# Sums of the output projection's weights formed in the first pass on GpSimd and loaded ready-made into the projection

## The chip, the cores and the metric

One Trainium2 chip, one core of it. The metric is device time in microseconds (us) of one execution of the whole program, the median of several executions. TensorE (PE) does the matmuls, VectorE (DVE), ScalarE (ACT) and GpSimd (POOL) the elementwise work, and all transfers are issued by SyncE (SP), one after the other.

## The reference, cut to what matters

Two layers of a decoder trunk over 2048 rows of 1024 columns, in fp32. Each layer normalises x, projects it, runs gated linear attention (GLA, 4 heads) and causal attention (MLA, 4 heads) beside each other, gates both, joins them and projects back onto x:

```
for l in range(2):
    h = rmsnorm(x, norm_g[l]);  u = h @ w_in[l]
    gla = rmsnorm(gla_mix(q, k, v, log_a)) * silu(g_gla)      # 512 columns, weighted by gla_norm_g
    mla = block_causal_attention(rope(q), rope(k), v) * silu(g_mla)   # 512 columns
    x = x + concat([gla, mla]) @ w_out[l]                     # w_out: 1024 x 1024
```

## The kernel before

A layer is four stages on the time line of the profile: a first pass over the rows (GLA; layer 0 from 0 to 345 us, layer 1 from 1152 to 1460), a second pass (gates and the MLA's projections, to 610 and 1730), the attention (`phase_b`, to 980 and 2107) and the output projection (`phase_c`, to 1152 and 2279). PE's order is written by hand in `block` and in the list of jobs of `phase_c`. The order of the other engines is set when the program is built, by a scheduler that puts each instruction where it reckons that its inputs are ready; on the chip every engine then takes its instructions strictly in that order, and SP issues its transfers in order too.

**The first pass** goes over 16 tiles of 128 rows in 8 pairs. A pair has six blocks of matmuls: `mi` (low-rank gates and latents) of both tiles, then `qk` and `v` of each. Beside them ACT and DVE make what the next matmuls need: `lah` and `ls_a` are the log gates, `ep`, `en`, `es` their exponentials, `kq` the scaled keys, `vs` and `vr` the values, `hT` the rounded rows. Every fp32 operand goes to PE as a high and a low part (`..._h`, `..._l`): ACT copies the high part, a second engine subtracts it to get the low one, and three matmuls (L97 to L99) make one product. In layer 0 ACT also sums the squares of later rows (`xn`, L405), each loaded into one buffer. GpSimd has nothing to do in this pass.

**The output projection** multiplies by the 2 x 2 blocks of `w_out` in Winograd's form of Strassen's method: seven products in place of eight, for each of two halves of the rows (p = 0, 1). Four products have sums of weight blocks as their weights: S1, N2, S3 and S4; two have a block itself (A11, A12), one has A22. A product is 48 matmuls of 128x512 (L1428, `co`). In p = 0 the order is M1 (A11), M2 (A12), M5 (S1), M6 (N2), M7 (S3), M3 (S4), M4 (A22). The sums are made in p = 0 itself: `s1`, `n2`, `s3`, `s4` load the blocks again (`ws`, 256 KB each), add them on DVE and POOL and split them with `wput` (L1204, L1205, L1207, L1208), one 128-row piece k after the other, a product or so ahead of their use. In the same stretch DVE also adds up the left operands: `y` (L1265 on ACT, L1266 on DVE), with `yr` and `rc` the stored rows and L1281 their sums, and takes the results out of PSUM (`xc`, L1333).

The names in the tiles: `kv` (matmuls from `vr` and `kq`) is the update of the GLA state, `od` the stored GLA output, `xt` rows loaded for later tiles, `osn` a staging tile.

## Time and profile before

| | |
|---|---|
| time, median of three runs | 2282.6 us (2280.12 to 2284.39) |
| time of the profiled execution | 2284.48 us |
| span in its profile | 2282.5 us |
| PE busy | 2205.2 us, 97% of the span |
| DVE busy | 1634.0 us, 72% |
| ACT busy | 1367.0 us, 60% |
| POOL busy | 422.2 us, 18% |
| granted clock of PE, mean | 0.989 |

The profile shows one execution; the span runs from the first instruction to the last, and 1.98 us of the execution's time lie outside it. Busy shares are means over stages with different limits, so the rows below are taken by stage.

### The profile page before, as it was taken

The numbers are of one execution on the slowest core, as the hardware profiler recorded it, in microseconds if no ns is written. First come the engines' busy times: TensorE is split into PE (matmuls) and PEld (weight loads), VectorE is DVE, ScalarE is ACT, GpSimd is POOL, SyncE is SP. The second block draws the span as 40 slices with busy tenths as digits, with TensorE's granted clock in tenths as the row PEclk, the third lists the DMA queues.
The fourth block names the chain that finished last, engine by engine and source line by source line (L and its number), as shares of the span: only waits on it lengthen the run. The fifth ranks groups of instructions, "written<-read, shape, count | busy, mean of one in ns | idle before, by whom it ended". The sixth has DMA issues, their size and how long they took to land.

```text
span 2282.5 us, 37395 instructions
## 1 busy us (share of the span) xinstructions
PE 2205.2 (97%) x12405; PEld 1899.2 (83%) x12405; DVE 1634.0 (72%) x4759; ACT 1367.0 (60%) x3706; POOL 422.2 (18%) x621
## 2 busy tenths in 40 slices
PE   7999999999999999998999999999999999999989
PEld 5778888888899988876878888888888989988677
DVE  5665557676788887677867667677777888885774
ACT  6655456776777777632445555667777777775321
POOL 0000002334312123224000000034342122122320
PEclk8999999999999999999999999999999999999999
DMA  5411114443411111168531011244434111111863
GB/s 192 134 48 42 43 51 145 133 136 101 137 37 51 31 47 52 47 222 268 176 107 41 29 42 43 64 151 140 124 100 125 29 54 36 39 55 48 271 217 112
DMA packets 180481, 223.66 MB, mean 98 GB/s; under 512 B 13936, under 2 KB 124608, under 8 KB 179264
## 3 DMA queue, kind: packets, MB, share of 16 engines
q1 hardware_dynamic: 180288, 221.28, 30.5%
q8 instruction: 98, 1.61, 0.3%
q14 instruction: 95, 0.78, 0.1%
HBM read 158.31 MB, written 62.91 MB: 97 GB/s over the span
## 4 chain that ended last, share of the span: by engine, by line
PE 81%; DVE 7%; ACT 5%; DMA 4%; issue 1%; SPq 1%; POOL 0%; ACTq 0%; DVEq 0%; POOLq 0%
PE co L1428 10%; PE tp L94 9%; PE o L1059 3%; PE sp L984 3%; PE o L1058 3%; PE sp L987 3%; PE o L1057 3%; PE sp L988 3%; PE sp L986 2%; PE sp L985 2%; PE mg L99 2%; PE mg L97 2%; PE mg L98 2%; PE gt L99 2%; PE gt L98 2%; PE gt L97 2%
## 5 line engine op out<-in xcount | busy, mean ns | idle before, releaser
L995 DVE TENSOR_SCALAR_CACHE_REDUCE p<-sp 128x512 f32<-128x512 f32 (+5 forms) x304 | 173.2, 573 | 23.1 <-PE sp L988 19.6
L1037 ACT ACTIVATE ph<-tp 128x512 fp32r<-128x512 f32 x224 | 130.7, 594 | 80.5 <-PE tp L94 70.3
L1038 DVE TENSOR_TENSOR pl<-tp,ph 128x512 fp32r<-128x512 f32 x224 | 152.2, 687 | 35.9 <-ACT ph L1037 34.8
L1002 ACT ACTIVATE p<-p,nm 128x128 f32<-128x128 f32 (+15 forms) x128 | 153.8, 1202 | 32.8 <-DVE nm L1001 27.5
L1057 PE MATMUL o<-ph,v 128*128 128x256 f32 x576 | 167.6, 291 | 3.6 <-ACT ph L1037 3.2
L1059 PE MATMUL o<-pl,v 128*128 128x256 f32 x576 | 170.0, 295 | 1.0 <-DVE pl L1038 0.5
L94 PE MATMUL tp<-cst,p 128*128 128x128 f32 x1088 | 168.0, 276 | 2.0 <-ACT p L1002 1.0
L1058 PE MATMUL o<-ph,v 128*128 128x256 f32 x576 | 161.4, 280 | 0.0
L184 POOL TENSOR_TENSOR ropeu<-kpe,cos 128x256 f32<-128x256 f32 x8 | 6.3, 791 | 808.6 <-DMA on<-od 433.2
L984 PE MATMUL sp<-kn,q 128*128 128x512 f32 (+3 forms) x320 | 129.6, 405 | 8.4 <-ACT q L919 6.7
L94 PEld LDWEIGHTS tp<-cst,p 128*128 128x128 f32 x1088 | 126.3, 141 | 11.2 <-ACT p L1002 2.2
L1057 PEld LDWEIGHTS o<-ph,v 128*128 128x128 f32 x576 | 109.1, 189 | 9.4 <-ACT ph L1037 4.6
L985 PE MATMUL sp<-kn,q 128*128 128x512 f32 (+3 forms) x320 | 116.6, 365 | 0.0
L986 PE MATMUL sp<-kn,q 128*128 128x512 f32 (+3 forms) x320 | 116.3, 370 | 0.0
L987 PE MATMUL sp<-kr,q 128*128 128x512 f32 (+3 forms) x320 | 115.2, 367 | 0.4
L1059 PEld LDWEIGHTS o<-pl,v 128*128 128x128 f32 x576 | 109.3, 190 | 6.5 <-DVE pl L1038 2.1
L1016 POOL TENSOR_SCALAR gt<-gt,rl 128x128 f32<-128x128 f32 x128 | 80.1, 636 | 185.5 <-DVE rl L1014 90.9
L988 PE MATMUL sp<-kr,q 128*128 128x512 f32 (+3 forms) x320 | 114.4, 368 | 0.0
L1058 PEld LDWEIGHTS o<-ph,v 128*128 128x128 f32 x576 | 109.1, 189 | 2.5
L97 PE MATMUL vp<-wv_h,hT 128*128 128x512 f32 x256 | 108.2, 423 | 1.8 <-ACT wv_h L264 1.8
L97 PE MATMUL qk<-wqk_h,hT 128*128 128x512 f32 x256 | 108.2, 423 | 0.0
L97 PE MATMUL mi<-wmi_h,hT 128*128 128x464 f32 x256 | 99.7, 390 | 7.4 <-ACT wmi_h L264 7.4
(322 smaller groups left out, 7061.8 us busy)
## 6 DMA issues: line engine op xcount, KB each, us to landing
rc<-yd SPq DMA_DIRECT2D x64, 256.0 KB, 4.6
ws<-in_w_out SPq DMA_DIRECT2D x56, 256.0 KB, 5.3
qd<-qs SPq DMA_DIRECT2D x32, 384.0 KB, 2.9
gst<-qd SPq DMA_DIRECT2D x64, 192.0 KB, 2.5
xn<-in_x SPq DMA_DIRECT2D x16, 512.0 KB, 3.3
od<-osn SPq DMA_DIRECT2D x32, 256.0 KB, 2.1
hf<-in_xt SPq DMA_DIRECT2D x16, 512.0 KB, 3.3
on<-od SPq DMA_DIRECT2D x32, 256.0 KB, 2.8
```

Of the source, the lines that this page charges most:

```text
L94: T.transpose(o, i, ident[:k, :k])
L97: T.matmul(o, lhsT=lh, rhs=rh, start=start, stop=False)
L984: T.matmul(o, lhsT=qn[:, 0, ts_], rhs=kn[:, 0, k0:k1], start=True, stop=False)
L985: T.matmul(o, lhsT=qn[:, 0, ts_], rhs=kn[:, 1, k0:k1], start=False, stop=False)
L986: T.matmul(o, lhsT=qn[:, 1, ts_], rhs=kn[:, 0, k0:k1], start=False, stop=False)
L987: T.matmul(o, lhsT=qrr[:, 0, ts_], rhs=kr[:, c0:c1], start=False, stop=False)
L988: T.matmul(o, lhsT=qrr[:, 1, ts_], rhs=kr[:, c0:c1], start=False, stop=True)
L995: V.tensor_scalar(out=pt[:, c0:c0 + w], in0=sp[:, 0:w], scalar1=0.0, scalar2=-3e38, op0=ALU.add, op1=ALU.max, accum_out=mx[:, m:m + 1])
L1057: T.matmul(o[:, s], lhsT=vh, rhs=ph[:, j, s], start=(kb == 0), stop=False)
L1058: T.matmul(o[:, s], lhsT=vl, rhs=ph[:, j, s], start=False, stop=False)
L1059: T.matmul(o[:, s], lhsT=vh, rhs=pl[:, j, s], start=False, stop=(last and j == 1))
L1428: T.matmul(o, lhsT=a[:, k, cs], rhs=y[:, b, :], start=(fresh and k == 0 and c == 0), stop=(k == 3 and c == 2), skip_group_check=True)
```

## The change

The four sums are no longer formed in the projection. Instead, the first pass of each layer forms them in 16 rounds, of one 128-row piece and 128 columns each, on GpSimd: three rounds in each of the pairs 1 and 2 and two in each of the pairs 3 to 7, as the code is written. A round loads the four blocks' pieces into one buffer `wq` (`wr_load`, two transfers of 128 KB), forms the sums in place (`wr_sum`, five POOL instructions), splits them into a high part (a copy on ACT) and a low part (POOL), and stores both to a new scratch tensor `wd` in device memory (`wr_put`, two transfers of 256 KB). There is one `wq` buffer, so a round's loads wait for the stores of the round before. In the projection `wsums` loads each sum's high and low parts, 1 MB each: S1 and N2 at the end of `phase_b`, S3 and S4 in the first two products. The A22 jobs move from the fifth product to the fourth. Apart from that the negated sine table `nsin` goes: `rope` now ends in a subtraction and an addition of half width on POOL where it had one addition, and the small tile `w3` takes the place of other staging tiles, with `finish_w3` of layer 1 called in the projection of layer 0.

```diff
-        V.tensor_scalar(out=nsin, in0=sin, scalar1=-1.0, scalar2=None, op0=ALU.mult)
...
-        eng.tensor_tensor(out=w[:, :, 0:32], in0=i[:, :, 32:64], in1=ns, op=ALU.mult)
+        eng.tensor_tensor(out=w[:, :, 0:32], in0=i[:, :, 32:64], in1=s, op=ALU.mult)
         eng.tensor_tensor(out=w[:, :, 32:64], in0=i[:, :, 0:32], in1=s, op=ALU.mult)
-        eng.tensor_tensor(out=o, in0=u, in1=w, op=ALU.add)
+        eng.tensor_tensor(out=o[:, :, 0:32], in0=u[:, :, 0:32], in1=w[:, :, 0:32], op=ALU.subtract)
+        eng.tensor_tensor(out=o[:, :, 32:64], in0=u[:, :, 32:64], in1=w[:, :, 32:64], op=ALU.add)
...
+        wrounds, wr = [(k, c) for k in range(4) for c in range(4)], {}
+
+        def wr_load(i):
+            k, c = wrounds[i]
+            wr[i] = w1.tile([P, 2, 4, P], F32R, tag="wq", name="wq", bufs=1)
+            t = wr[i][:, 0].bitcast(F32)
+            for half in range(2):
+                r0 = half * 512 + k * P
+                dma(t[:, 2 * half:2 * half + 2, :],
+                    w_out[l][r0:r0 + P, :].rearrange("p (a b c) -> p a b c", a=2, b=4)[:, :, c, :])
+
+        def wr_sum(i):
+            t = wr[i][:, 0].bitcast(F32)
+            a11, a21, a12, a22 = (t[:, j, :] for j in range(4))
+            G.tensor_scalar(out=t[:, 0:2, :], in0=t[:, 0:2, :], scalar1=sm["glag"], scalar2=None, op0=ALU.mult)
+            G.tensor_tensor(out=a22, in0=a21, in1=a22, op=ALU.add)
+            G.tensor_tensor(out=a21, in0=a11, in1=a21, op=ALU.subtract)
+            G.tensor_tensor(out=a11, in0=a11, in1=a22, op=ALU.subtract)
+            G.tensor_tensor(out=a12, in0=a12, in1=a11, op=ALU.add)
+
+        def wr_put(i):
+            k, c = wrounds[i]
+            w = wr.pop(i)
+            A.activation(out=w[:, 1], in_=w[:, 0].bitcast(F32), func=AF.Copy)
+            G.tensor_tensor(out=w[:, 0], in0=w[:, 0].bitcast(F32), in1=w[:, 1].bitcast(F32), op=ALU.subtract)
+            for part in range(2):
+                dma(wd[l][:, part, :, k, c * P:(c + 1) * P], w[:, part].bitcast(F32))
...
+            for b0 in () if p == 0 else (0, 2, 4) if p < 3 else (0, 4):
+                i = wnext[0]
+                wnext[0] += 1
+                wj[b0] = {1: [go(wr_load, i)], 6: [go(wr_sum, i)]}
+                wj[b0 + 1] = {5: [go(wr_put, i)]}
...
             load_a1(1)
+            for name in ("S1", "N2"):
+                wsums(l, name)
...
+    def wsums(l, name):
+        b = ("N2", "S3", "S4", "S1").index(name)
+        wo[name] = unit([P, 4, 512], F32R, f"{name}h{l}"), unit([P, 4, 512], F32R, f"{name}l{l}")
+        for part in range(2):
+            dma(wo[name][part].bitcast(F32), wd[l][:, 1 - part, b])
...
-        def s1(k):
-            wmake("S1")
-            t, u = wload(1, k), wload(1, 4 + k)
-            V.scalar_tensor_tensor(out=u, in0=t, scalar=g, in1=u, op0=ALU.mult, op1=ALU.add)
-            wput("S1", k, u, G)
...
-        for j, f in enumerate((s1, n2, s3, s4, a22)):
-            for k in range(4):
-                at(0, j, k, go(f, k))
+        at(0, 0, 0, go(wsums, l, "S3"))
+        at(0, 1, 0, go(wsums, l, "S4"))
+        for k in range(4):
+            at(0, 3, k, go(a22, k))
```

In the program that is built, the rounds do not stand where the code has them. Three places show it. First ACT, at the end of the fourth pair of layer 1's first pass. Before, the last rows of the log gates (`lah`) are followed by the values (`vs`, `vr`) that the next `kv` matmuls take:

```order
L398 ACTIVATE xn<-xt 128x1024
L120 ACTIVATE ls_a<-ls_a 128x256
L509 ACTIVATE qkT<-tp 128x512
L512 ACTIVATE kq<-qkT 128x256
L456 ACTIVATE lah<-ls_a 128x256
L532 ACTIVATE vs<-vp,rt 128x512
L534 ACTIVATE vr<-vp,rt 128x512
L349 ACTIVATE hT<-xt 128x512 x2
L471 ACTIVATE ep<-bp 128x256
L472 ACTIVATE en<-bp 128x256
```

Now the copy of the sixteenth and last round stands between them:

```order
L399 ACTIVATE xn<-xt 128x1024
L121 ACTIVATE ls_a<-ls_a 128x256
L510 ACTIVATE qkT<-tp 128x512
L513 ACTIVATE kq<-qkT 128x256
L457 ACTIVATE lah<-ls_a 128x256
L617 ACTIVATE wq<-wq 128x512
L533 ACTIVATE vs<-vp,rt 128x512
L535 ACTIVATE vr<-vp,rt 128x512
L350 ACTIVATE hT<-xt 128x512 x2
L472 ACTIVATE ep<-bp 128x256
L473 ACTIVATE en<-bp 128x256
```

The row L617 is the only one that is new here. Of the 16 copies of layer 1, the first stands behind the first `lah` of the pass and this one behind the eighth; in layer 0 the first stands behind the first `lah`, the ninth behind the fourth `hT` pair and the sixteenth ahead of the seventh `vs`.

Second SP, in the first pass of layer 1. Before, it issues rows and GLA outputs alone (`xt`, `od`):

```order
L59 DMA xt<-xd_80 128x1024
L59 DMA od_114<-osn 128x512
L59 DMA od_115<-osn 128x512
L59 DMA xt<-xd_80 128x1024 x2
L59 DMA od_116<-osn 128x512
L59 DMA od_117<-osn 128x512
L59 DMA xt<-xd_80 128x1024
L59 DMA xt<-xd_81 128x1024
```

Now the loads and stores of the rounds stand between them, each `wq` load behind the `wd` stores of the round before and each `wd` store behind the copy on ACT and the subtraction on POOL:

```order
L59 DMA wq<-in_w_out 128x2x128 x2
L59 DMA wd_102<-wq 128x4x128 x2
L59 DMA xt<-xd_79 128x1024
L59 DMA wq<-in_w_out 128x2x128 x2
L59 DMA od_115<-osn 128x512
L59 DMA wd_102<-wq 128x4x128 x2
L59 DMA wq<-in_w_out 128x2x128 x2
L59 DMA wd_102<-wq 128x4x128 x2
L59 DMA wq<-in_w_out 128x2x128 x2
L59 DMA od_116<-osn 128x512
```

Every other row of this queue is now one whose turn comes only when a round has got that far.

Third DVE, at the start of layer 0's projection. Before, three `y` low parts stand ahead of the first results (`xc`), with the scaling of `ws` for S1 between them:

```order
L1069 TENSOR_TENSOR yT<-o,gT 128x256
L1266 TENSOR_TENSOR y<-rc,y 128x512 x3
L1333 TENSOR_TENSOR xc<-co,xc 128x512
L1221 SCALAR_TENSOR_TENSOR ws<-ws,pk 128x512
L1333 TENSOR_TENSOR xc<-co,xc 128x512 x2
L1221 SCALAR_TENSOR_TENSOR ws<-ws,pk 128x512
L1333 TENSOR_TENSOR xc<-co,xc 128x512
L1266 TENSOR_TENSOR y<-rc,y 128x512
L1266 TENSOR_TENSOR y<-yr,y 128x512
L1281 TENSOR_TENSOR yr<-rc,yr 128x512
```

Now the `ws` rows are gone, and the four results of M1 stand ahead of the first `y`:

```order
L1107 TENSOR_TENSOR yT<-o,gT 128x256
L212 TENSOR_TENSOR w3r<-w_12285,w3r 32x256
L1349 TENSOR_TENSOR xc<-co,xc 128x512 x4
L1282 TENSOR_TENSOR y<-rc,y 128x512 x4
L1282 TENSOR_TENSOR y<-yr,y 128x512
L1297 TENSOR_TENSOR yr<-rc,yr 128x512
L1282 TENSOR_TENSOR y<-yr,y 128x512
L1297 TENSOR_TENSOR yr<-yr,rc 128x512
L1297 TENSOR_TENSOR yr<-rc,yr 128x512
```

The first `y` (L1282, L1266 before) is what M2 waits for; it has moved behind four results.

## Rows read from the trace of the kernel before

**Rows 1.** Windows over the projections' first halves, one second half and one first pass.

```profile
core 0: us, PE busy (x) PEld busy (x) DVE busy (x) ACT busy (x) POOL busy (x), PEclk, DMA share, GB/s
980.00:1075.60 95.60, 84.32 (x340) 66.10 (x339) 70.44 (x91) 29.63 (x49) 36.28 (x24) 0.93 0.81 264
2107.20:2202.40 95.20, 82.73 (x339) 64.50 (x339) 72.52 (x92) 29.91 (x49) 35.72 (x24) 0.95 0.80 258
2202.40:2278.60 76.20, 76.20 (x337) 62.80 (x335) 41.00 (x65) 14.54 (x23) 0.00 (x0) 1.00 0.40 132
1168.00:1309.00 141.00, 137.39 (x755) 115.69 (x754) 94.92 (x305) 77.42 (x253) 0.00 (x0) 1.00 0.11 34
```

**Rows 2.** Waits from 975 to 1100 us: engine, line, releaser, us, times, longest.

```profile
PE co L1428 <- DVE S4l L1205: 4.0, 1, 4.0
...
PE co L1428 <- DVE S3l L1208: 2.5, 1, 2.5
...
PE co L1428 <- ACT y L1265: 1.6, 1, 1.6
```

**Rows 3.** Windows right behind two of these waits, columns as in rows 1.

```profile
1003.70:1017.00 13.30, 12.95 (x48) 9.91 (x49) 13.30 (x19) 3.71 (x7) 4.56 (x3) 0.87 0.96 296
1047.80:1062.00 14.20, 10.17 (x36) 8.20 (x36) 9.80 (x12) 5.03 (x9) 7.10 (x6) 0.76 0.83 250
```

**Rows 4.** DVE by form, 980 to 1076 us: count, busy us, mean ns, idle before.

```profile
L1333 DVE TENSOR_TENSOR xc<-co,xc 128x512 f32<-128x512 f32 x25 | 16.5, 678 | 2.0 <-PE co L1428 2.0
```

**Rows 5.** POOL by form over the span, columns as in rows 4.

```profile
L1016 POOL TENSOR_SCALAR gt<-gt,rl 128x128 f32<-128x128 f32 x128 | 80.1, 636 | 185.5 <-DVE rl L1014 90.9 <-DMA gt<-gd 39.3 <-PE tp L94 25.6
...
L187 POOL TENSOR_TENSOR ropew<-qr,nsin 128x128 f32<-128x128 f32 x32 | 23.7, 741 | 0.0
...
L1205 POOL TENSOR_TENSOR N2l<-ws,N2h 128x512 fp32r<-128x512 f32 x8 | 12.0, 1494 | 17.7 <-ACT N2h L1204 17.7
...
L1205 POOL TENSOR_TENSOR S1l<-ws,S1h 128x512 fp32r<-128x512 f32 x8 | 11.0, 1370 | 67.8 <-ACT S1h L1204 67.8
...
L187 POOL TENSOR_TENSOR ropew<-kpe,nsin 128x128 f32<-128x128 f32 x8 | 3.7, 461 | 0.0
```

**Rows 6.** DMA issues of tiles xd, then gt: issue to landing, us.

```profile
DMA to landing us min/median/max: 2.5/4.1/7.5
DMA to landing us min/median/max: 1.7/1.9/6.1
```

**Rows 7.** DMA issues from 1152 to 1300 us: KB each, median us to landing.

```profile
xd<-xc SPq DMA_DIRECT2D x1, 256.0 KB, 2.8
```

**Rows 8.** ACT by form, 65 to 121 us, columns as in rows 4.

```profile
L349 ACT ACTIVATE hT<-xt 128x512 fp32r<-128x512 f32 x6 | 3.4, 622 | 0.0
```

**Rows 9.** Timeline of ACT, layer 1: start, us, instruction, idle before and releaser.

```profile
1168.17 0.39 ACT L421 ACTIVATE jk<-mi 128x256 f32<-128x256 f32 x1 [0.92 <-DVE lr L417]
...
1306.37 0.40 ACT L456 ACTIVATE lah<-ls_a 128x256 fp32r<-128x256 f32 x1
1308.91 0.69 ACT L532 ACTIVATE vs<-vp,rt 128x512 f32<-128x512 f32 x1 [2.15 <-PE vp L99]
```

**Rows 10.** Timeline of ACT, layer 0.

```profile
69.69 1.06 ACT L405 ACTIVATE xn<-xn 128x1024 f32<-128x1024 f32 x1 [2.30 <-DMA xn<-in_x]
...
74.13 1.06 ACT L405 ACTIVATE xn<-xn 128x1024 f32<-128x1024 f32 x1 [3.29 <-DMA xn<-in_x]
...
117.96 1.14 ACT L349 ACTIVATE hT<-xt 128x512 fp32r<-128x512 f32 x2
...
186.86 0.69 ACT L532 ACTIVATE vs<-vp,rt 128x512 f32<-128x512 f32 x1 [2.39 <-PE vp L99]
```

**Rows 11.** Waits from 65 to 121 us.

```profile
ACT xn L405 <- DMA xn<-in_x: 16.7, 11, 3.3
```

**Rows 12.** Timeline of DVE, then of PE, around one update of the GLA state.

```profile
1267.91 0.69 DVE L535 TENSOR_TENSOR vr<-vs,vr 128x512 fp32r<-128x512 f32 x1 [1.44 <-ACT vr L534]
...
1269.83 0.28 PE L97 MATMUL kv<-vr,kq 128*128 128x256 f32 x1
```

More of the change, by code (lines that the diff above doesn't have):

```diff
@@ L76, in trunk @@
     sin = cp.tile([P, NT, 32], F32, name="sin")
-    nsin = cp.tile([P, NT, 32], F32, name="nsin")
     v3 = cp.tile([P, NT, 3], F32, name="v3")
@@ L86, in trunk @@
     yd = [dp.tile([P, KT, QD], F32, name=f"yd{q}") for q in range(NQD)]
+    wd = [dp.tile([P, 2, 4, 4, 512], F32, name=f"wd{l}") for l in range(DEPTH)]
     qd = [dp.tile([P, HEADS, 2, 192], F32, name=f"qd{g}") for g in range(NG)]
@@ L202, in layer_small @@
         r["gqk"] = lp.tile([P, 1], F32, name="gqk")
-        w3 = lp.tile([96, 256], F32, name="w3", bufs=1)
+        w3 = w3[0:96, 0:256]
         dma(w3, w3s[l])
@@ L659, in pass1 @@
                 dma(cst[:, 0:C_MASK], consts[:, 0:C_MASK])
-                layer_small(0)
+                layer_small(0, w1.tile([P, 512], F32, tag="osn", name="w3"))
                 for load, _ in pq:
@@ L726, in run @@
                 ts_ = slice(4 * b, 4 * b + 4)
-                rope(G, w2, kpe[:, ts_, :], kpe[:, ts_, :], 4, cos[:, ts_, :], sin[:, ts_, :], nsin[:, ts_, :],
+                rope(G, w2, kpe[:, ts_, :], kpe[:, ts_, :], 4, cos[:, ts_, :], sin[:, ts_, :],
                      "qr")
@@ L1183, in phase_c @@
             layer_g8(l + 1)
-            layer_small(l + 1)
+            layer_small(l + 1, wc.tile([P, 512], F32, tag="rc", name="w3", bufs=3))
+            smalls[l + 1]["finish_w3"]()
         g = smalls[l]["glag"]
```

40 lines of the change are left out of this document (12 added, 28 removed).

## The prediction

> **What bounds the kernel now.** I read the windows by stage first, then the waits inside the one stage that loses time, and last the order in which the trace's instructions will stand once the rounds are among them. In layer 1's first pass PE is busy 137.4 of 141 us, with POOL at 0 and ACT busy 77 [rows 1]: PE is the bound there, the others have room. In the second half of layer 1's projection PE is busy 76.20 of 76.20 us for seven products [rows 1], which is 10.89 us a product. The first half is the same work, but takes 95.6 us in layer 0 and 95.2 in layer 1 [rows 1]: 19.4 and 19.0 us are lost, 38.4 in all. The waits name what ends last there: S4's low part 4.0 us, S3's 2.5, the left operand y 1.6 [rows 2]. PE is busy for 84.3 us with work that needs 76.2 [rows 1]; the other 8 us are the clock, granted at 0.87 and 0.76 in the stretches right behind the stalls [rows 3], between its two levels of 1.2 and 2.4 GHz.
>
> **What the change takes away.** The sums leave the projection: S3's and S4's waits have no maker on DVE left, and what DVE, ACT and POOL did for them goes too, with 24 loads of 256 KB a layer; eight of 1 MB come, four of them issued before the half begins. I do not book all 38.4 us. Three things are late next. M2: DVE now takes M1's four results ahead of the first y, four rows of 0.68 us at a spacing of some 0.6 [rows 4]; that is 2.4 us, of which some 1.4 fall on PE. S4's low part is now a load that waits for M1's end, and SP holds a row for M2 behind it: about 1.0. M5's y is still made on DVE: 1.6 was lost before [rows 2]; I take 2.5, since results now stand between its rows. Each stall brings a lower clock: at 0.87 over 13.3 us that is 1.7 us, at 0.76 over 14.2 it is 3.4 [rows 3]; I take 3.5 for two milder drops. Left are 8.4 us a half, so the gain is 11.0 and 10.6; less 1 us, because the y copies on ACT now stand among the last of the attention's. Together **20 us**. The bounds: 10, if M5 and S3's load stay as late as S3 and S4 are now, and 37, if nothing of the kind is left.
>
> **What it adds in the first pass.** Sixteen rounds a layer, and they form a closed loop, because one buffer serves them all: the loads wait for the stores, the stores for POOL, POOL for the loads. No round stands in the trace of before, so I add one up from the nearest rows.
> - The subtraction that makes the low part, 128x512 on POOL: 1.43 us, between 1.37 and 1.49 [rows 5].
> - The store of 256 KB in runs of 512 bytes: the tile xd is stored in the same shape, 2.8 us when it is alone [rows 7], 2.5 at least [rows 6]; loaded stretches give up to 7.5, and I take 3.3 for a high end, since this pass moves only 34 GB/s [rows 1].
> - The first load, 128 KB: 64 KB in runs of 512 bytes land in 1.9 us [rows 6], 256 KB in 2.8; I take 2.2 (1.9 to 2.7). The second runs beside it and beside the scaling.
> - The scaling on POOL, 128x256: 128x128 takes 0.64 [rows 5]; I take 1.0 (0.64 to 1.1).
> - Four 128x128 operations, each on the result of the one before: 0.46 or 0.74 [rows 5], so 2.4 with 0.60 each (1.85 to 2.96).
> - ACT's copy of 128x512: 0.62 [rows 8].
> - Six hand-overs. A row load that follows ACT shows the size: from 69.69 + 1.06 to 74.13 are 3.38 us [rows 10] for a landing of about 3.3 us, so below 0.1 each; 0.4 in all.
>
> Sum: 1.43 + 2.8 + 2.2 + 1.0 + 2.4 + 0.62 + 0.4 = **10.8 us a round**, with 9.3 and 12.5 as ends. This would be hidden if the copies stood far enough apart in ACT's order, since ACT waits in that order. They don't. In layer 1 the first stands just ahead of the row at 1168.17 and the sixteenth ahead of that at 1308.91 [rows 9]: 140.7 us for 15 rounds, 9.4 each. In layer 0 the ninth stands behind the hT pair that ends at 119.1 and the sixteenth ahead of 186.86 [rows 10]: 67.8 us for 7, 9.7 each; before the ninth they stand further apart. Behind a late copy are queued the values, the gates and the keys of the tile at hand, and PE's next kv matmuls wait for the values: vr is ready at 1268.60 and used at 1269.83 [rows 12], so the slack is 1.2 us, once. A PE that is 97% busy in this stretch makes nothing up.
> - Layer 1: 15 x 10.8 - 140.7 - 1.2 = 20.1 us lost.
> - Layer 0: 7 x 10.8 - 67.8 - 1.2 = 6.6 us lost.
> - Another 2 us in layer 0 before the ninth round: SP stands still between a store and the next load, with row loads (xn) queued behind it, and ACT already waits for those 11 times, 16.7 us in all [rows 11]. That is also the nearest case of the same mechanism: a loop of one buffer, 4.4 us long, that holds ACT each time it comes round.
>
> Together **28.7 us**. It hangs on the round: one microsecond of it is 22 us of time. Costed at nothing: POOL's own 16 x 4.8 = 77 us a layer, since the engine is idle here; ACT's 16 x 0.62 us a layer, at a load of 55%; DVE's slowing beside POOL in rows of 0.4 to 0.7 us, as long as it stays under the slack of 1.2; the smaller rope rows, w3 and the 4 MB of stores and loads in quiet stretches.
>
> Against the round's length stands a figure of the Trainium skill ("GPSIMD Engine Reference", section 3.1, Elementwise — side-by-side cycle accounting): an addition of 2048 fp32 columns takes 4497 ns there. My estimate from it is 0.28 us for 128 columns and 1.12 for 512, which would make the round about 9.2 us long. The rows for 128 columns, 0.46 and 0.74, don't agree; the page's figure is for one long operation.
>
> **The sum.** 2284.5 - 20 + 28.7 = 2293.2 for the profiled execution. That one lies 1.9 us above the median of the runs, so 2291.3 as a median, **2291 us**: slower by 8 us, 0.4%. A measurement of this kernel can tell 0.2%, 4.6 us, from no change.
>
> **Rivals.**
> - *The rounds fit.* The POOL rows cost what the cheapest show (0.46) and the landings their least, 9.3 to 10.2 us a round. Then layer 0 loses 0 to 4 us and layer 1 some 3 (9.4 is a mean, with shorter gaps in it) to 11; the time is 2282.6 - 20 + 3 to 15 = 2266 to 2278. For it: POOL is otherwise idle here and DMA nearly so. Against it: DVE is busy two thirds of this stretch [rows 1], and POOL's rows vary with it. It decides from about 10.4 us a round downwards, where loss and gain are equal. The page of the Trainium skill named above would put the round here; its figure is no part of this chance. Chance 0.27.
> - *The projection gives back nearly all.* The rounds take 10.8 us, but the stalls at M2 and M5 don't come: 37 gained, 28.7 lost, 2274. For it: PE has no wait at all in the second half. Against it: y is made on DVE as before. Chance 0.06.
> - *The rounds are long*, 11.8 us and more, because POOL and DVE slow each other and other rows of SP (xt, od) come between a store and its load: at 12, layer 1 loses 38 us, layer 0 17, and the time is 2282.6 - 20 + 55 = 2318. Chance 0.12.
> - *The change does little in the projection*: S3 and S4 are loaded late and take the place of the sums as the last to come; 10 gained, 28.7 lost, 2301. Against it: no load of 1 MB has to wait for more than one product. Chance 0.05.
> - My forecast, a round of 10.3 to 11.8 us, holds 0.50: 2280 to 2313.
>
> **How the numbers follow.** The likeliest case gives 2291. Slower by over 0.2% are the forecast from 10.6 us a round upwards (0.40), the long rounds and the weak projection: 0.57. Faster are the rounds that fit and the full gain in the projection: 0.33. The forecast's shortest rounds, 10.3 to 10.6, give no change: 0.10. The range runs from a little under the rounds that fit, 2264, to rounds of 12 us, 2318; it leaves out longer ones.
>
> **What the profile of the changed kernel would show.** Right: the rows of L617 on ACT with an idle time before them that is released by POOL, in most rounds; 16 of them evenly 10.3 to 11.8 us apart in layer 1; PE waiting in its first pass for vr, lah or kq, where it now hardly waits; the pass of layer 1 about 20 us longer; the first halves of the projections at 84 to 87 us, with y and no S3 or S4 among the waits. Wrong: L617 without idle time before it, or rounds as far apart as the order has them, 9.4 us. The POOL rows L609 to L612 decide the size: at 0.46 I am too slow, at 0.9 too fast. What would break the prediction altogether is a slack on ACT's side that I don't see, or a projection that still waits for its weights.

## The result and the profile after

The changed kernel takes 2309.7 us (median of four runs, 2301.63 to 2311.47) against 2283.45 us (2280.12 to 2284.39) for the kernel before, run beside it: ratio 1.0111, 95% interval 1.0084 to 1.0137. It is slower by 1.1%, inside the range that was given, and on the side that was thought likeliest, but 19 us above the predicted 2291. The profiled execution took 2311.47 us, with a span of 2309.6 us, 27.1 more than before.

Where do those 27.1 us lie? The stages end at rows that both traces have (the last `kv` of a first pass, the first `sp` of an attention, the first and the last `co` of a projection). By these rows the first passes of the kernel before end at 374 and 1498 us and its second passes at 596 and 1719; the 345, 1460, 610 and 1730 given with the stages above were rough. In us:

| | first pass 0 | second 0 | attention 0 | projection 0 | first pass 1 | second 1 | attention 1 | projection 1 |
|---|---|---|---|---|---|---|---|---|
| before | 374.4 | 221.6 | 384.1 | 171.7 | 345.8 | 221.6 | 388.0 | 170.8 |
| after | 396.2 | 225.8 | 383.7 | 166.0 | 368.3 | 222.1 | 385.9 | 157.1 |
| difference | +21.8 | +4.2 | -0.4 | -5.7 | +22.5 | +0.5 | -2.1 | -13.7 |

The windows of after, with the columns of [rows 1], give the first halves of the two projections, layer 1's first pass from the first of its rounds, and layer 0's second pass:

```profile
core 0: us, PE busy (x) PEld busy (x) DVE busy (x) ACT busy (x) POOL busy (x), PEclk, DMA share, GB/s
1005.70:1095.50 89.80, 81.28 (x338) 64.92 (x339) 46.16 (x70) 21.01 (x35) 8.35 (x6) 0.96 0.79 257
2148.00:2229.50 81.50, 78.80 (x338) 64.19 (x339) 47.33 (x69) 20.40 (x34) 9.32 (x7) 0.98 0.82 259
1188.10:1309.30 121.20, 106.14 (x538) 88.38 (x538) 76.58 (x215) 63.07 (x194) 47.99 (x66) 0.93 0.32 98
396.20:622.00 225.80, 223.01 (x1078) 189.79 (x1077) 155.54 (x368) 154.08 (x413) 90.01 (x144) 0.99 0.39 124
```

The projections' first halves are 5.8 and 13.7 us shorter than in [rows 1]. In the first pass PE was busy 137.4 of 141 us (97%) at a granted clock of 1.00; now it is busy 106.1 of 121.2 (88%) at 0.93. What PE waits for there, in the whole of layer 1's first pass (engine, line, releaser, us, times, longest):

```profile
PE at L524 <- ACT qkT L510: 5.5, 4, 2.8
PE kv L98 <- ACT vr L535: 5.3, 2, 3.6
PE kv L99 <- DVE vr L536: 3.4, 3, 2.1
PE lg L454 <- ACT lrT L449: 3.2, 3, 1.3
PE tp L95 <- DVE qkp L482: 1.2, 1, 1.2
```

Three quarters of what is listed, 14.0 of 18.6 us, end with ACT; the longest is for `qkT`, which ACT copies too. What holds ACT is in the view of the tile `wq` over both layers (min/median/max ns of one; below, the idle time before its instructions, and who waited for them):

```profile
L608 POOL TENSOR_SCALAR wq<-wq,pk x32: 924/927/1763, 28.2 to 1348.6; 128x256 f32<-128x256 f32 x32
L609 POOL TENSOR_TENSOR wq<-wq x32: 453/461/801, 29.9 to 1349.6; 128x128 f32<-128x128 f32 x32
...
L617 ACT ACTIVATE wq<-wq x32: 627/632/655, 32.1 to 1351.9; 128x512 fp32r<-128x512 f32 x32
L618 POOL TENSOR_TENSOR wq<-wq x32: 1264/1289/1569, 32.8 to 1352.6; 128x512 fp32r<-128x512 f32 x32
...
  DMA wq<-in_w_out: 346.1, 37
  POOL wq L612: 65.2, 29
...
DMA to landing us min/median/max: 2.3/2.5/7.5
```

29 of the 32 copies (L617) are preceded by idle time of ACT that POOL's last sum ends, 65.2 us in all over both layers. The timeline of ACT shows their pace; these are the ninth and the last of layer 0 and four of layer 1, its first, fifth, sixth and last:

```profile
131.20 0.64 ACT L617 ACTIVATE wq<-wq 128x512 fp32r<-128x512 f32 x1 [0.25 <-POOL wq L612]
...
209.50 0.63 ACT L617 ACTIVATE wq<-wq 128x512 fp32r<-128x512 f32 x1 [3.91 <-POOL wq L612]
...
1188.11 0.63 ACT L617 ACTIVATE wq<-wq 128x512 fp32r<-128x512 f32 x1 [1.36 <-POOL wq L612]
...
1231.84 0.63 ACT L617 ACTIVATE wq<-wq 128x512 fp32r<-128x512 f32 x1 [3.15 <-POOL wq L612]
...
1242.17 0.63 ACT L617 ACTIVATE wq<-wq 128x512 fp32r<-128x512 f32 x1 [2.09 <-POOL wq L612]
...
1351.90 0.63 ACT L617 ACTIVATE wq<-wq 128x512 fp32r<-128x512 f32 x1 [1.64 <-POOL wq L612]
```

In layer 1 they stand (1351.90 - 1188.11) / 15 = 10.92 us apart, where the order of before left 9.4 for each [rows 9]. One round on POOL's timeline, between the fifth and sixth copy, shows what the loop is made of:

```profile
1232.54 1.28 POOL L618 TENSOR_TENSOR wq<-wq 128x512 fp32r<-128x512 f32 x1 [0.74 <-ACT wq L617]
1239.03 0.93 POOL L608 TENSOR_SCALAR wq<-wq,pk 128x256 f32<-128x256 f32 x1 [5.20 <-DMA wq<-in_w_out]
1240.04 0.46 POOL L609 TENSOR_TENSOR wq<-wq 128x128 f32<-128x128 f32 x1
...
1241.67 0.47 POOL L612 TENSOR_TENSOR wq<-wq 128x128 f32<-128x128 f32 x1
```

Low part 1.28, then 5.2 us in which the stores land and the next piece is loaded, scaling 0.93, four sums to 1242.14, and the copy at 1242.17: 10.3 us from copy to copy, of which POOL works 4.1. Over layer 1's 15 rounds the time between a low part and the next scaling is 5.5 us in the mean.

In the projections, PE's waits answer to [rows 2]. In layer 0, then in layer 1:

```profile
PE co L1445 <- ACT y L1281: 4.7, 2, 3.7
PE co L1445 <- DVE xc L1349: 3.4, 2, 2.7
PE co L1445 <- DVE y L1282: 0.2, 1, 0.2
...
PE co L1445 <- ACT y L1281: 2.5, 1, 2.5
PE co L1445 <- DVE y L1282: 0.2, 1, 0.2
```

No S3 and no S4 stands among them. The `y` that PE waits longest for in layer 0, in M2, is not the first one, as the reading of DVE's order above had it, but the fourth; and its maker ACT waits for a load of rows:

```profile
1029.75 0.63 ACT L1281 ACTIVATE y<-rc 128x512 fp32r<-128x512 f32 x1 [10.70 <-DMA rc<-yd]
```

That load was issued at 1019.77 us, 2.7 us behind the second megabyte of S4 (`S4l`, issued at 1017.08, landed 10.6 us later), and landed 9.9 us after its issue, behind it. In the kernel before the same load took 5.3 us.

### The profile page after: what moved, and what is told of

It is laid out like the page before. It is cut to its first block, busy times and chain, and to the rows that moved or that the text cites. A ratio compares the mean times of both kernels' runs of the same rounds, so it can differ in the third digit from the quotient of the medians.

```text
span 2309.6 us, 37795 instructions
## 1 busy us (share of the span) xinstructions
PE 2216.6 (96%) x12405; PEld 1908.1 (83%) x12405; DVE 1606.9 (70%) x4718; ACT 1363.0 (59%) x3706; POOL 509.6 (22%) x813
## 4 chain that ended last, share of the span: by engine, by line
PE 74%; DMA 10%; POOL 5%; ACT 5%; DVE 3%; issue 2%; SPq 1%; POOLq 0%; ACTq 0%; DVEq 0%
PE co L1445 12%; PE tp L95 8%; DMA wq<-in_w_out 4%; DMA wd<-wq 3%; PE sp L1022 3%; PE sp L1025 3%; PE o L1097 3%; PE sp L1024 2%; PE sp L1023 2%; PE o L1096 2%; PE sp L1026 2%; PE o L1095 2%; PE mg L100 2%; PE mg L98 2%; PE mg L99 2%; PE gt L100 2%
## 5 line engine op out<-in xcount | busy, mean ns | idle before, releaser
L1076 DVE TENSOR_TENSOR pl<-tp,ph 128x512 fp32r<-128x512 f32 x224 | 152.2, 687 | 32.7 <-ACT ph L1075 31.5
L939 POOL TENSOR_SCALAR gst<-kpe,rk 128x64 f32<-128x64 f32 x128 | 55.3, 446 | 275.2 <-DVE rk L111 108.4
L608 POOL TENSOR_SCALAR wq<-wq,pk 128x256 f32<-128x256 f32 x32 | 34.4, 1076 | 342.9 <-DMA wq<-in_w_out 342.9
```

## The experiments

The theory: a round is a loop of about 11 us through one buffer, ACT's copies were ordered closer than that, and ACT, which works strictly in its order, stands still at each; so most of the loss goes if ACT isn't in the loop, though the loop stays. The rival: the rounds' work itself (POOL beside DVE, transfers) costs the time, wherever the copy is made. Ratios are against the kernel before, run beside it. The differences by stage, taken as in the table above, are those from before. Each is read from one profiled execution, so 1 or 2 us in a single stage say little:

| | ratio (95%) | first 0 | second 0 | attention 0 | projection 0 | first 1 | second 1 | attention 1 | projection 1 |
|---|---|---|---|---|---|---|---|---|---|
| after | 1.0111 (1.0084-1.0137) | +21.8 | +4.2 | -0.4 | -5.7 | +22.5 | +0.5 | -2.1 | -13.7 |
| rounds only | 1.0225 (1.0209-1.0240) | +21.8 | +4.2 | +0.5 | 0.0 | +22.4 | +0.6 | -1.1 | +0.8 |
| loads only | 0.9960 (0.9946-0.9975) | +9.8 | +4.2 | -2.5 | -5.7 | -0.5 | +0.7 | -2.6 | -15.1 |
| copy in its place | 0.9976 (0.9967-0.9985) | +9.3 | +2.5 | +1.8 | -11.6 | +6.3 | +0.5 | -3.3 | -13.8 |
| copy on POOL | 0.9967 (0.9951-0.9983) | +9.9 | +2.8 | -0.8 | -11.7 | +6.8 | +0.7 | -2.5 | -13.7 |
| layout only | 1.0019 (1.0009-1.0028) | +2.1 | +4.2 | +0.2 | +1.5 | -0.2 | +0.6 | -2.6 | 0.0 |
| w3's homes | 0.9975 (0.9961-0.9988) | +12.2 | +0.6 | -0.7 | -11.5 | +7.7 | +0.6 | -1.9 | -14.0 |
| loads later | 0.9969 (0.9957-0.9980) | +12.1 | +0.7 | +0.4 | -12.7 | +7.9 | +0.5 | -2.7 | -12.6 |
| "from pair 2" | 0.9972 (0.9961-0.9984) | +15.5 | +0.6 | -2.1 | -12.3 | +7.2 | +0.6 | -2.8 | -13.5 |
| second pass | 1.0136 (1.0111-1.0161) | +1.2 | +21.9 | +8.2 | -9.5 | -0.4 | +20.6 | +5.6 | -13.4 |
| no sums | 1.0000 (0.9990-1.0009) | +10.4 | +2.7 | +0.8 | -6.1 | +8.5 | +0.6 | -2.3 | -13.8 |
| attention | 0.9919 (0.9899-0.9939) | -1.2 | +0.7 | +3.9 | -9.2 | +1.1 | +0.7 | -0.5 | -14.9 |
| own queue | 0.9995 (0.9984-1.0007) | +13.1 | +2.5 | +1.1 | -4.8 | +6.3 | +0.6 | -3.2 | -15.0 |

**The rounds alone.** The changed kernel with the projection of before; `wd` is written and not read.

```diff
-            for name in ("S1", "N2"):
-                wsums(l, name)
...
-        at(0, 0, 0, go(wsums, l, "S3"))
-        at(0, 1, 0, go(wsums, l, "S4"))
-        for k in range(4):
-            at(0, 3, k, go(a22, k))
+        for j, f in enumerate((s1, n2, s3, s4, a22)):
+            for k in range(4):
+                at(0, j, k, go(f, k))
```

> The changed kernel with its sixteen rounds a layer, but the projection forms the sums itself as before and the stored sums are not read. Theory (the one-buffer loop holds ACT, and PE behind it): both first passes stay longer by 22 us, the second pass of layer 0 by 4, and the first halves of the projections are back at 95 us: about 2283 + 48 = 2331 us. If a good part of the 22 us comes from the projection's own changes (w3, the A22 jobs), it is under 2320.

2332.93 us (2331.97 to 2334.2). The losses of the first passes and of layer 0's second pass are there whole, and the projections take their old time: loss and gain add, to within 2 us a stage.

**The loads alone.** No rounds; eight plain stores of 1 MB a layer fill `wd`, and the projection loads from it (so it multiplies by other weights). In the program that is built, layer 1's stores are issued from 1113 to 1127 us, in layer 0's projection, so layer 1's first pass has neither rounds nor stores.

```diff
-            for b0 in () if p == 0 else (0, 2, 4) if p < 3 else (0, 4):
+            for b0 in () if p == 0 else (0, 4) if p == 1 else (0,):
...
-                wj[b0] = {1: [go(wr_load, i)], 6: [go(wr_sum, i)]}
-                wj[b0 + 1] = {5: [go(wr_put, i)]}
+                wj[b0] = {1: [go(wr_fill, i)]}
```

> The other half alone: no rounds; eight stores of 1 MB a layer fill the scratch tensor with another weight in the first pass, and the projection loads from it as in the changed kernel, so its weights are not the sums. Theory: the first passes and the second pass of layer 0 are as before (within 2 us each), the projections gain 6 and 14 to 15 us: about 2283 - 21 = 2262 us. If the projection gains because it starts later or in another state of the queues, it is above 2272.

2272.83 us (2269.81 to 2275.48), 11 us above the 2262 expected. The projections gain 5.7 and 15.1, close to the changed kernel's 5.7 and 13.7. Of the miss, layer 0's first pass has most: the stores were issued between 22.8 and 29.8 us, among the loads of the first weights, and PE waits once for 10.7 us there. That is this experiment's own, not the change's. The other 4.2 stand in the second pass of layer 0, where no round runs.

**The copy in its place.** ACT makes the copies at the place that the code gives them, not where the scheduler moves them.

```diff
-            A.activation(out=w[:, 1], in_=w[:, 0].bitcast(F32), func=AF.Copy)
+            tc.keep_in_program_order(A.activation(out=w[:, 1], in_=w[:, 0].bitcast(F32), func=AF.Copy))
```

> The changed kernel with ACT's copy of each round kept where the code has it, so that the copies stand 14 us apart in the pairs 1 and 2 and some 21 us in the pairs 3 to 7; POOL's work, the transfers and the copies are the same. Theory (the loop of 10.9 us holds ACT because the copies stand 9.4 us apart): they hardly wait now, the first passes lose at most 3 us each, and the time is about 2283 - 21 + 4 + 4 = 2270 us. Rival (POOL's work beside DVE and the added transfers slow the first pass, whoever waits): the passes stay 22 us longer each, 2310 us.

2277.29 us (2271.86 to 2280.67), 33 us less than the rival has. ACT now waits for POOL before 7 copies, 7.8 us in all, where it was 29 and 65.2; two copies in a row of layer 1:

```profile
1278.36 0.64 ACT L617 ACTIVATE wq<-wq 128x512 fp32r<-128x512 f32 x1 [0.90 <-POOL wq L612]
1297.17 0.62 ACT L617 ACTIVATE wq<-wq 128x512 fp32r<-128x512 f32 x1
```

The first passes still lose 9.3 and 6.3 us, not the 3 at most that were expected.

**The copy on POOL.** ACT is out of the loop.

```diff
-            A.activation(out=w[:, 1], in_=w[:, 0].bitcast(F32), func=AF.Copy)
+            G.tensor_copy(w[:, 1], w[:, 0].bitcast(F32))
```

> The changed kernel with the copy made on POOL in place of ACT, so that no engine that PE needs is in the loop; the rounds stay as close as the scheduler sets them. Theory: PE no longer sees the loop, except where SP holds a row load behind a store; the first passes lose 0 to 5 us each: 2266 to 2276 us. Rival (POOL beside DVE): POOL has 16 more operations a layer, so the passes lose 22 us each or more: 2310 us.

2274.97 us (2272.44 to 2279.65). The copies now run on POOL from 1168.45 to 1334.95, (1334.95 - 1168.45) / 15 = 11.1 us apart: the loop is as long as before, and POOL, whose only work it is, waits in it. With ACT out of it the first passes lose 9.9 and 6.8 us in place of 21.8 and 22.5, more than the 0 to 5 expected. The rival would have left them where they were; it falls for 12 and 16 us of the loss, and stays possible for the rest.

**The layout alone.** The kernel before with only the small edits of the change (no `nsin`, the shorter rotation, `w3` in a buffer of `osn` and later of `rc`).

```diff
-                layer_small(0)
+                layer_small(0, w1.tile([P, 512], F32, tag="osn", name="w3"))
...
-            layer_small(l + 1)
+            layer_small(l + 1, wc.tile([P, 512], F32, tag="rc", name="w3", bufs=3))
+            smalls[l + 1]["finish_w3"]()
```

> The kernel before with only the small edits of the change beside the rounds: no negated sine and the shorter rotation, and w3 read into a buffer of osn in the first pass of layer 0 and into one of rc in the projection. No round, no wd, and the projection makes the sums as before. Theory (a moved memory layout costs time by itself): in the changed kernel, layer 0's uq of the second pass lies over the two buffers of osn, so its ACT copy waits some 3.7 us for the last osn store, and the second pass of layer 0 takes 225.8 us from its start to the first score of phase B and not 221.6, +4; w3 in a buffer of rc holds up the projection's first y by 0 to 3. Sum: 2287 to 2290. Rival (the 4 us come from the rounds, as a stage that ends with its queues fuller): 2283, as before.

2289.56 us (2284.55 to 2290.7), as the theory has it: 2.1 in the first pass, 4.2 in the second, 1.5 in the projection, all in layer 0, against a gain of 2.6 in layer 1's attention. ACT's timeline of the changed kernel has the place where the second pass loses its time:

```profile
406.94 1.12 ACT L284 ACTIVATE uq<-stg,pk 128x384 fp32r<-128x384 f32 x2 [3.73 <-DMA od<-osn]
```

The weights of the second pass (`uq`) wait for a store out of the first pass's staging tile. In the program that is built, `uq` covers the bytes 195456 to 207744 of a partition, and `osn`'s two buffers in layer 0 begin at 200320 and 202368; `w3` was the first tile that took such a buffer, which moved both up in the pool. In layer 1 they begin at 218400 and 220448, and there is no wait.

**Other homes for w3.** From the kernel with the copy on POOL.

```diff
-                layer_small(0, w1.tile([P, 512], F32, tag="osn", name="w3"))
+                layer_small(0, w1.tile([P, 1024], F32, tag="wq", name="w3", bufs=1))
...
-            layer_small(l + 1, wc.tile([P, 512], F32, tag="rc", name="w3", bufs=3))
+            layer_small(l + 1, wc.tile([P, 512], F32, tag="ws", name="w3", bufs=4))
```

> The kernel with the copy on POOL (2274.97), and w3 in other buffers: in layer 0's first pass it is the first tile of wq's buffer (in use only from the second pair on), so that osn's buffers lie past uq's end, and in the projection it takes a buffer of ws (which the first products don't need) in place of one of rc. Theory (address overlap): the 3.7 us wait of uq for the last osn store is gone, the second pass of layer 0 is 222 us again, and the projection's start in layer 0 gains 0 to 3: 2268 to 2272. Rival (the wait only shows a queue that is late anyway, and the next step waits in its place): 2275.

2276.79 us (2274.42 to 2282.8). The wait of `uq` is gone and the second pass is back at 222.2 us, so the overlap was its cause; but the first pass of layer 0 takes 2.3 us more, layer 0's projection gains nothing further, and the sum is the same. The time is that of the rival, the mechanism that of the theory.

**Loads later.** S3 and S4 are loaded one product later each.

```diff
-        at(0, 0, 0, go(wsums, l, "S3"))
-        at(0, 1, 0, go(wsums, l, "S4"))
+        at(0, 1, 0, go(wsums, l, "S3"))
+        at(0, 2, 0, go(wsums, l, "S4"))
```

> As the one with w3's new homes, and the 2 MB of the ready S3 and the 2 MB of S4 are loaded one product later each (at the start of the second and of the third product, not of the first and the second). S3 is used from the fifth product of the half, S4 from the sixth. Theory (in the projection after layer 0 PE waits 3.7 us in the second product for a y whose load stands behind these 2 MB in the queue, and 2.7 us at the third product's xc): 3 to 6 us less in layer 0, 0 to 2 in layer 1, so 2262 to 2268. Rival (those operands are late because their stores or the DMA rings are, not for the place in the queue; or the later loads make S3 and S4 late): the time of the run with w3's new homes, or 2 to 5 us more.

2276.72 us (2274.42 to 2278.91): 1.2 less in layer 0's projection, 1.4 more in layer 1's. A miss, but it does not test its theory, because the edit hardly moved the loads: SP's order is made by the scheduler. This is S4's low part in layer 0's projection without the edit, then with it:

```profile
1003.36 0.33 SPq L59 DMA_DIRECT2D S4l<-wd  x1
...
1004.68 0.33 SPq L59 DMA_DIRECT2D S4l<-wd  x1
```

The projections' first `co` start at 992.2 and 993.3, so it is issued 11.2 and 11.4 us behind them; S3's high part is issued 2.2 us ahead of them both times, and S4's high part alone moved, by 2.4 us.

**Rounds "from pair 2".**

```diff
-            for b0 in () if p == 0 else (0, 2, 4) if p < 3 else (0, 4):
+            for b0 in () if p < 2 else (0, 2, 4) if p < 6 else (0, 4):
```

> As the one with the later loads, and the 16 rounds stand in pairs 2 to 7 (three in each of pairs 2 to 5, two in 6 and 7) and not in pairs 1 to 7. What the first pass still loses with the copy on POOL is 9.9 us in layer 0 and 6.8 in layer 1. Theory A (in layer 0 most of it is lost between 107 and 160 us, where the first rounds meet the last splits of the layer's weights on ACT and DVE): 3 to 6 less in layer 0 and about nothing in layer 1, 2257 to 2264. Theory B (each round costs some 0.4 to 0.6 us wherever it stands): the same time as the run with the later loads, within 1.5 us.

2276.57 us (2275.58 to 2278.39). It cannot tell one theory from the other, because the edit did not move the rounds: POOL's first sums ran at 30.1 us here and at 29.9 without the edit, its last low part at 224.6 and 221.3. Only PE's order is held to the code; POOL and SP take the rounds as early and as densely as the loop lets them. For layer 0 the trace with the copy on POOL decides against theory B. The window goes from 159 us to the end of the rounds:

```profile
159.00:217.60 58.60, 58.60 (x329) 50.06 (x327) 36.61 (x99) 26.77 (x88) 26.09 (x35) 1.00 0.35 105
```

PE is not idle at all there, although the last five rounds run: those cost nothing. The 9.9 us are lost before, in a stretch where PE has waits without any round too (it is busy 107.6 of 119 us from 30 to 149 us in the kernel before).

**The rounds in the second pass.** From the kernel with the later loads; the rounds' functions are moved to the second pass and their tile to its pool.

```diff
+            for i in range(16):
+                for n, f in ((0, wr_load), (5, wr_sum), (12, wr_put)):
+                    n += 8 + 15 * i
+                    at(n // 32, n // 8 % 4, n % 8, go(f, i))
```

> As the kernel with w3's new homes and the later loads (2276.7), but the 16 rounds of a layer are made in its second pass, one every 15 steps of the blocks, and none in the first; w3 of layer 0 has a tile of its own in the first pass. Theory (what the rounds still cost comes from the first pass, whose waits for ACT and DVE end last there, and where DVE's busy time grows from 238.1 to 251.1 us with POOL at work beside it): in the second pass PE waits for nothing (221.3 of 221.6 us busy) and DVE is busy 155 of 222 us, so the rounds are hidden; the first passes take 344 and 346 us again, the projections keep their 12 and 13, phase B its 1 to 2.5: 2252 to 2258. Rival (POOL, already busy 87 us there with the rotations, holds up the queries): the second passes lose 5 to 8 each, 2264 to 2272.

2318.2 us (2313.36 to 2321.29), far beyond the rival as well. The first passes are whole again (+1.2 and -0.4), and the second ones lose 21.9 and 20.6. The window of layer 0's, and PE's waits in it and in the attention's first 40 us:

```profile
375.60:619.10 243.50, 229.19 (x1078) 191.88 (x1077) 177.27 (x368) 151.76 (x413) 175.10 (x249) 0.98 0.53 162
...
PE sp L1019 <- DVE mx L1027: 12.6, 1, 12.6
PE qp L98 <- POOL lh L746: 4.6, 3, 2.2
```

PE used to be busy 221.3 of 221.6 us here. DVE goes from 154.7 us to 177.3, and the queries' own POOL work (`lh`, the rotations) now comes behind rounds that wait for their loads. PE's direct waits for POOL are 6.0 of the 14.3 us that it is idle; that the rest, and the attention's late first scores, come from the same cause is likely, but not shown. It looks like the first pass's error again, with POOL in ACT's place.

**No sums.** The copy on POOL, with the scaling and the four sums left out.

```diff
         def wr_sum(i):
-            t = wr[i][:, 0].bitcast(F32)
...
-            G.tensor_tensor(out=a12, in0=a12, in1=a11, op=ALU.add)
+            pass
```

> As the kernel with the copy on POOL (2274.97), but the rounds leave out the scaling and the four sums: wd gets the plain weights as high and low parts, so the projection multiplies by the weights and not by their sums. Loads, stores, the copy and the low part stay. Theory (the 9.9 and 6.8 us that the first passes still lose come from POOL's work beside DVE, whose transfers between SBUF tiles go from 683 to 780 ns): POOL does 16 x 1.7 us less than half of it, so the loss falls to 3 to 6 in layer 0 and 2 to 4 in layer 1: 2265 to 2270. Rival (the rounds' loads and stores, 8 MB a layer with both, delay the first pass's own loads): 2273 to 2276.

2285.65 us (2281.55 to 2288.58), above the rival's time too. With 31.8 us of POOL's work in layer 1's first pass instead of 81.5 the loss is 8.5 us, not less than 6.8: the theory of POOL's work falls as it was put. It is not refuted altogether, since DVE is still 9.4 us busier than before, where it was 13.0 with the sums; what POOL still does slows DVE most (see the last section). The rounds also run closer together, (1298.03 - 1172.42) / 15 = 8.4 us, so they load the pass more while they last. Of the 9.3 us by which the stages are longer than with the sums, layer 0's projection, the same code in another order of DVE, has 5.6: it gains 6.1 and not 11.7.

**Own queue.** The copy on POOL, with the rounds' transfers issued by POOL.

```diff
-                dma(t[:, 2 * half:2 * half + 2, :],
-                    w_out[l][r0:r0 + P, :].rearrange("p (a b c) -> p a b c", a=2, b=4)[:, :, c, :])
+                G.dma_start(out=t[:, 2 * half:2 * half + 2, :],
+                            in_=w_out[l][r0:r0 + P, :].rearrange("p (a b c) -> p a b c", a=2, b=4)[:, :, c, :])
...
-                dma(wd[l][:, part, :, k, c * P:(c + 1) * P], w[:, part].bitcast(F32))
+                G.dma_start(out=wd[l][:, part, :, k, c * P:(c + 1) * P], in_=w[:, part].bitcast(F32))
```

> As the kernel with the copy on POOL (2274.97), with the rounds in the first pass, but the rounds' loads and stores are issued from POOL's queue and not from SP's. Theory (what the first passes still lose, 9.9 and 6.8 us, comes from SP: its in-order queue stands 57.4 us before the rounds' stores for the copy, 32.7 before their loads for the store to land and 13.0 for the low part, and the first pass's own loads and stores are behind them): the losses fall to 2 to 5 in layer 0 and 1 to 3 in layer 1, 2263 to 2269. Rival (they come from POOL's and the DMA engines' work beside DVE, whose busy time in layer 1's pass goes from 238.1 to 251.1 us): 2272 to 2278; POOL's own time for issuing, which no run here shows, would add to that.

2283.77 us (2275.9 to 2287.1). In layer 1's first pass SP no longer waits for a round at all (its waits for `wq`, 57.4, 13.0 and 32.7 us with the copy on POOL, are gone); POOL waits in its stead:

```profile
POOL wq L602 <- DMA wd<-wq: 32.5, 8, 7.9
POOL wq L608 <- DMA wq<-in_w_out: 16.2, 8, 3.7
```

Yet the pass loses 6.3 us, hardly less than 6.8, although eight of its sixteen rounds now run ahead of it, in the projection; layer 0's loses 13.1. So the loss does not need SP to stand still for the rounds. What POOL's issuing itself costs is not separated: the rows take 0.7 to 0.8 us each, and the copies are now 15 us apart.

**The rounds in the attention.** As in the second pass, but with a round from the start of one of the attention's longer steps to the start of the next; `yT` has one buffer and not two, for the memory.

```diff
+                if k - 1 in wat:
+                    wr_sum(wat.index(k - 1))
+                    wr_put(wat.index(k - 1))
+                if k in wat:
+                    wr_load(wat.index(k))
...
-                yT = bpl.tile([P, QG], F32, name="yT")
+                yT = bpl.tile([P, QG], F32, name="yT", bufs=1)
```

> As the one with the rounds in the second pass, but they are made in phase B, one beginning at each of the first 16 of its 32 steps that have g from 3 to 7 and ending at the start of the next step; yT has one buffer and not two, to make room. In phase B PE is busy 375.6 of 384.1 us and DVE 310, mostly on transfers out of PSUM. Theory (DVE's transfers out of PSUM keep their time beside POOL, and nothing of phase B waits for POOL but the gates): 2253 to 2260. Rival (a gate's scaling on POOL comes behind a round's sums and holds up values, or yT's single buffer does): phase B 5 to 10 longer in each layer, 2265 to 2275.

2267.41 us (2265.3 to 2271.54): the fastest of all, 0.8% faster than the kernel before and 42 us faster than the changed one. The windows of layer 0's attention and of layer 1's first pass:

```profile
595.50:983.50 388.00, 377.27 (x2610) 343.55 (x2608) 317.11 (x1109) 272.63 (x724) 160.94 (x271) 0.99 0.32 94
1146.00:1492.90 346.90, 342.48 (x1862) 289.64 (x1861) 237.66 (x755) 193.18 (x613) 0.00 (x0) 1.00 0.18 57
```

The first pass has its old time again to within 1.2 us, and the attention takes 73 us more of POOL's work for 3.9 us in layer 0 and, beside the 2 to 3 us that layer 1's gains in most of the other kernels, some 2 there. Layer 0's projection gained 9.2 us, where 12 were expected. Together these are most of why it came out at 2267 and not at 2253 to 2260.

## Why the prediction was right, and where it was off

**The round: right, in part by luck.** 10.8 us were worked out, 10.92 measured. The POOL rows, the copy and the hand-overs took 5.4 us (5.85 taken): low part 1.29 (1.43), scaling 0.93 (1.0), four sums some 2.2 with their gaps (2.4), copy 0.63 (0.62). Stores and loads took 5.5 (5.0). The two errors cancel; either alone is some 10 us of time by the forecast's own count. So the sign given for the size did not hold: the sums' rows came at 0.46, and yet the round was no shorter than forecast. The estimate of 0.28 and 1.12 us from the Trainium skill ("GPSIMD Engine Reference", section 3.1) does not agree: the POOL rows show 0.46 for 128 columns and 1.29 for 512.

**Layer 1's first pass: right.** 20.1 predicted, 22.5 measured; with 10.92 the forecast's own formula gives 21.9. The two experiments on the copy show that the mechanism is the one forecast, ACT's place in the loop and not the loop's length alone, for 16 of the 22.5 us. PE did not wait for `lah` or `kq`, but for `qkT` and `vr`, which stand behind the copies in the same way.

**Layer 0's first pass: the step that was off.** 8.6 us were predicted, 21.8 lost. After the ninth copy the formula holds: the copies stand (209.50 - 131.20) / 7 = 11.2 us apart where the order left 9.7, 10.5 us in all and 9.3 after the slack, for 6.6 predicted. The error lies before it. "Before the ninth they stand further apart" was put at 2 us; the ninth copy came at 131.20 and not at 119.1, 12 us late. The copies up to it stand (131.20 - 32.08) / 8 = 12.4 us apart. The order of before left 11.2 there, from the end of the pass's first `lah` to 119.1:

```profile
28.89 0.42 ACT L456 ACTIVATE lah<-ls_a 128x256 fp32r<-128x256 f32 x1 [1.12 <-DVE ls_a L121]
```

So a round of 10.8 us would have fitted, as the forecast had it, and one of layer 0's did not. Of the 1.5 us that these are longer than layer 1's, 0.7 are the landing of the stores, while the layer's weights and rows come in, and 0.4 two copies (the third and the seventh) that ACT itself reached late; the rest is spread over loads and POOL's rows. I had looked at what the order leaves between the copies, and not asked how long a round takes in a stretch that moves so much more. How much of the 12 us the loop alone makes is not shown, since with ACT out of it layer 0 still loses 9.9, nearly all in this stretch.

**The projections: the sum right, its parts not.** 20 predicted; 5.7 and 13.7 measured, 19.4. S3 and S4 are gone from the waits, and y and the results are next, as said. In layer 0 y comes 4.7 us late (1.4 and 1.0 for M2 were taken), and M5 loses 3.4 more at a result (2.5 taken); in layer 1 only 2.5 is left. Of M2's two reasons the smaller one was the right one: not DVE's four results ahead of the first y, but the row load behind S4, which was put at 1.0. So the first halves take 89.8 and 81.5 us, one above and one below the 84 to 87 that were to show the forecast right; that the sum came out is luck. Several experiments gain 11 to 13 us in layer 0's projection with the same code there, others 5 to 10. Part of that is the order of DVE, which the scheduler made anew for each program. The first result of M2 (`xc`) stands six rows (`y` and `yr`) behind M2's last `y` in the changed kernel and four rows behind it with the copy on POOL; these are the row ahead of it and the result, in the one and in the other:

```profile
1034.03 0.69 DVE L1282 TENSOR_TENSOR y<-yr,y 128x512 fp32r<-128x512 f32 x1
1034.63 0.68 DVE L1349 TENSOR_TENSOR xc<-co,xc 128x512 f32<-128x512 f32 x1
...
1017.15 0.69 DVE L1297 TENSOR_TENSOR yr<-yr,rc 128x512 f32<-128x512 f32 x1
1017.75 0.68 DVE L1349 TENSOR_TENSOR xc<-co,xc 128x512 f32<-128x512 f32 x1
```

In all four kernels with the first order (the changed one, no sums, the attention, own queue) PE's longest wait for a result there is 2.6 to 2.7 us; in the others that load ready-made sums it is 0.7 to 1.4. The row load of M2 also lands later, 24.0 us after the first `co` in the changed kernel and 22.0 with the copy on POOL, with waits for y of 3.7 and 2.0 us; why it does stays open.

**"Costed at nothing": wrong in two places.** The layout with `w3` in `osn`'s buffers takes 2.1 us more in layer 0's first pass and 4.2 in its second, and both are there without a single round; of the 4.2 the overlap is shown to be the cause, of the 2.1 nothing is. And with ACT free the first passes still lose 9.9 and 6.8 us. In layer 1 with the copy on POOL, the windows over the rounds and behind them show that it falls while they run:

```profile
1152.00:1337.00 185.00, 177.06 (x947) 147.12 (x946) 133.08 (x380) 95.03 (x300) 81.26 (x112) 0.99 0.37 115
1337.00:1504.60 167.60, 166.87 (x919) 141.54 (x918) 118.04 (x376) 98.66 (x313) 0.27 (x1) 1.00 0.21 67
```

PE is idle 7.9 us in the first and 0.7 in the second; the whole pass of before leaves 4.9. In layer 0 it falls before 159 us alone, and later rounds cost nothing. DVE is busier by 8 to 22 us in the first pass of every kernel that has rounds there, and within 1 us of before in those without; the last section shows that POOL's work does this. But the loss does not go with it: in layer 1 DVE is 13.0, 15.9, 9.4 and 8.1 us busier with the copy on POOL, in its place, without the sums and with the own queue, and the losses are 6.8, 6.3, 8.5 and 6.3. That DVE's lateness is what PE meets is likely, but not shown, and what sets the size of this rest stays open.

**The sum.** First passes +44.3 for 28.7, second pass +4.2 for 0, projections -19.4 for -20, attention and the rest -2: 27.1 us of span against 8.7 predicted. Of the 18.4 between them layer 0's first pass holds 13.2 and the layout of the second pass 4.2. That the time still lies in the range is due to the range, which had rounds of 12 us at its end. None of the rivals came whole: in layer 1 a round of 10.9 us is not a long one, and the projection gave what it was said to; but in layer 0 the mean of all 15 distances, (209.50 - 32.08) / 15, is 11.8 us, where the long rounds begin.

## What to carry to other kernels

A loop over one buffer has a length of its own, and every engine that works strictly in order and takes part in it is paced by it: compare the loop with the distance at which the built program, not the code, puts its steps, stretch by stretch, and take that loop's length from the stretch it runs in. Keep the loop on an engine that has nothing else to do there, or in a stage with slack: with the same sixteen rounds a layer takes 22 us more in the first pass through ACT, 7 to 10 with POOL alone, 21 in the second pass where POOL is needed (and 6 to 8 in the attention behind it), and 2 to 4 in the attention. An edit of the code moves such a loop only on an engine whose order is held to the code: two experiments here left the program nearly as it was, and the rows of the trace say so before the time does. A small tile that takes another's buffer can move that buffer under the next stage's first tile; a wait for a store across a change of pools shows it.
